# Queued work moved by some ticks, and sums split in halves, in a one-core decoder layer

## The chip, the core and the metric

The kernel is one launch on one core of a Trainium2 chip. Its engines are named as in the profile: PE is TensorE's matrix unit and PEld its weight load, DVE is VectorE, ACT is ScalarE, POOL is GpSimd, and SP issues transfers. SPq, ACTq and POOLq are the transfer queues of these engines. The metric is the device time of one execution in microseconds; lower is better.

## What is computed

One layer of a decoder, for 256 prompt rows and 8 sample rows of one new token each, 264 rows in all, with 2048 channels, in float32:

```python
proj = x @ w_in                                   # 2048 -> all mixer parts
y_a  = ssd(z, conv(xbc), dt, h0)                  # Mamba-2 scan, 32 heads, 4 groups; new state is an output
y_b  = sc_b * dwconv3(sc_c * sc_h)                # short gated convolution
mix  = sigmoid(g_a)*(y_a @ w_branch_ssd) + sigmoid(g_b)*(y_b @ w_branch_sc)
x1   = LN(ALPHA*x + mix @ w_out)
q    = x1 @ w_q                                   # 8 heads, product keys 128 x 128 = 16384 experts
idx, gate = top16 of the sums of two top16 lists, softmax
x2   = LN(ALPHA*x1 + sum_k gate_k * gelu(x1 . u[idx_k]) * v[idx_k])
y    = x2 + sigmoid(x2 @ ple_gate_w) * (p @ ple_proj_w)
```

For 208 of the 264 rows (the "dense" rows, TD = 208) the kernel multiplies x1 with all 16384 rows of u and of v and lays a mostly-zero matrix of gates between the two products; for the other 56 rows (the "sparse" rows, 8 sample rows and 48 prompt rows, shared over 56 gather columns) it gathers the chosen rows of u and v.

## The kernel before

**Weights.** Every product is fed by 128x2048 blocks of weights that come by SP's queue into three tiles (`w`). A half block, 128x1024, is split into a rounded upper part `whi` by ACT (L158) and the rest `wlo` by DVE (L159). PE multiplies both. Four buffers of each part exist up to the stage that scores the keys, five after it, so the two splitting engines can run four to five halves ahead of PE. In the first stages a half is 24 matmuls of 264 columns (L255, L256, L257); in the u and v stages it is 16 matmuls, eight of 416 columns on `whi` (L293 and, for the last block row, L296) and eight of 208 columns on `wlo` (L294).

**Ticks.** The program is written as a list of instructions by Python code that walks through the half blocks. Each half ends with `tick`: functions put down by `defer(n, f)` run n ticks after, and background work, written as generators, goes on. A generator that yields a number spends it from a budget of about 1.1 to 1.3 a tick; one that yields `("w", n)` sleeps n ticks. So the place of every background instruction between the splits of two halves, on each engine's own queue, is set by these numbers. Each engine takes its queue in order.

**Stages**, with the count of halves: convolved inputs (48), short convolution (96), z (32), the two branch products, w_out, w_q (to half 368), u (256 halves, 368 to 624), v (256 halves in eight chunks of 16 blocks), the small product with p (four halves, L1559 to L1561), and the last gate (32).

**What the change touches.**
- `ssd_group` (L551): the scan of one group. L592 takes an exponential of 1024 columns, L595 eight times a relu of 128 columns for each of two chunks, and L598 an exponential again, all on ACT.
- `ssd_samples` (L643): 64 units, one per tick, over a ring of eight buffers `h0t`. A unit's state is loaded by SP's queue, one tick later scaled by ACT (L681), then added to on DVE (L675), then multiplied with C (L665), and stored by POOL's queue in the fourth tick after the load.
- `Norm` (class at L856): the layer norm over the 16 blocks of 128 channels. `pilot` (L874) multiplies the first block with ones for an estimate of the mean; `gather` (L881) takes it off every block and makes the products; `rest` (L923) does the same for the 56 sparse rows, one of 16 blocks after another (L948 on ACT, L952 on DVE), each waiting for that block's `gather`.
- `select` (L1134): the choice of 16 experts per row on DVE, its transposes on PE (L1220, `slt`), `gates` (L1256) which makes the gate matrix from products (`g_mm`, L1279) and stores it to `g_d`.
- `sparse_experts` (L1285): gathers of u's and v's rows by POOL (`ug`, two buffers), a multiply of 2048 columns per gather on DVE (L1363 for u, L1373 for v), and `replicate` (L1304), which lays out x1 by transposes (`x1t`).
- `to_v` (L1517): once the gates are stored and nothing is deferred, it closes the pools of the selection, opens those for v, and starts `prep(0)` (L1432: loads `gl` and `al`, two multiplies, the split `co`) and `residual` (L1495: 16 copies of x1 into `acc`, L1499).
- `v_evac` (L1474): adds each finished product of the v stage to `acc` (L1480, 416 columns: two halves of 208). In the last chunk the two halves of `acc` are folded into one (L1482), and the block goes to the second norm.

## Time and profile before

| what | value |
| --- | --- |
| runs | 2478.10, 2481.56, 2488.36 us; median 2481.56 us |
| the profiled execution | 2488.03 us, of which the span is 2486.3 us |
| mean granted TensorE clock | 0.994 of full speed |
| HBM read, written | 646.32 MB, 39.46 MB, 276 GB/s over the span |
| busy share PE, DVE, ACT, POOL | 98%, 81%, 59%, 24% |

The page of the profile gives busy times and the chain of work that ended last. Beside it stand: the list of waits (`PE mm L294 <- DVE wlo L159: 23.9, 35, 2.8` says that PE's line L294 waited 23.9 us in all, 35 times, 2.8 us at the longest, for DVE's L159); windows, which give each engine's busy time and instructions in a stretch, then the granted clock, the share of the DMA engines, and GB/s; groups of instructions (line, engine, operation, shapes, count | busy us, mean ns of one | idle before it); and the timeline (start, duration, engine, line, operation, and in brackets the idle time before it and what ended it).

### The profile page before, as it was taken

The page shows a single profiled execution, that of the slowest core. Times are in us where ns is not written, and L with a number is a line of the kernel's source. Part 1 is how long each engine was busy: PE and PEld are TensorE (multiplying, and loading weights), DVE is VectorE, ACT ScalarE, POOL GpSimd, SP SyncE. Part 2 cuts the span into 40 slices and gives each one's busy share as a digit, 9 for nine tenths or more (in the row PEclk, how much of TensorE's full clock was granted, in tenths as well). Part 3 has the DMA queues.
Part 4 walks back from the last instruction along what each step waited for, and adds up shares of the span by engine and source line. Part 5 has one row for each costly group of instructions (what it writes and reads, how often), then busy time and mean ns, then how long its engine had stood idle before and what let it go on. Part 6 is the DMA issues. An engine that isn't in the chain of part 4 may idle for free.

```text
span 2486.3 us, 47938 instructions
## 1 busy us (share of the span) xinstructions
PE 2427.8 (98%) x19049; PEld 2399.4 (97%) x19049; DVE 2008.8 (81%) x3192; ACT 1459.5 (59%) x2310; POOL 606.5 (24%) x720
## 2 busy tenths in 40 slices
PE   9999999999999999999999999999999999999989
PEld 9999999999999999998999999999999999999989
DVE  8889865567455578999998778769899999899987
ACT  6776654455444455754777788866544555445564
POOL 2332200000000010100345666632332323323201
PEclk9999999999999999999999999999999999999999
DMA  6788755555555555566779999999999999999554
GB/s 250 250 293 277 256 190 189 199 194 189 201 188 202 190 201 187 195 211 202 243 290 341 357 360 371 370 348 399 394 371 381 383 378 395 364 372 379 200 176 148
DMA packets 137105, 688.91 MB, mean 277 GB/s; under 512 B 15744, under 2 KB 53168, under 8 KB 63280
## 3 DMA queue, kind: packets, MB, share of 16 engines
q1 hardware_dynamic: 89168, 495.46, 55.9%
q0 software_dynamic: 28688, 158.69, 16.5%
q10 hardware_dynamic: 19024, 31.69, 3.5%
q8 instruction: 149, 2.44, 0.4%
q14 instruction: 76, 0.62, 0.1%
HBM read 646.32 MB, written 39.46 MB: 276 GB/s over the span
## 4 chain that ended last, share of the span: by engine, by line
PE 57%; DMA 15%; DVE 15%; issue 6%; ACT 6%; POOL 1%; ACTq 0%; SPq 0%; DVEq 0%; POOLq 0%
PE mm L255 12%; PE mm L257 12%; PE mm L256 12%; PE mm L293 10%; DVE wlo L159 7%; DMA w<-vP 6%; PE mm L294 5%; DMA w<-uT 4%; ACT whi L158 3%; DMA h0t<-h 2%; DVE ug L1363 1%; ACT o L1270 1%; DVE acc L1480 1%; DMA o_hs<-h0t 1%; DMA ug<-vR,sidx 1%
## 5 line engine op out<-in xcount | busy, mean ns | idle before, releaser
L159 DVE TENSOR_TENSOR wlo<-w,whi 128x1024 fp32r<-128x1024 f32 x916 | 1112.3, 1222 | 359.7 <-ACT whi L158 354.1
L158 ACT CAST whi<-w 128x1024 fp32r<-128x1024 f32 x916 | 943.8, 1044 | 611.8 <-DMA w<-vP 249.8
L293 PE MATMUL mm<-x,whi 128*128 128x416 f32 x1920 | 572.8, 365 | 4.1 <-ACT whi L158 4.1
L293 PE MATMUL mm<-co,whi 128*128 128x416 f32 x1920 | 562.1, 361 | 0.0
L255 PE MATMUL mm<-x,whi 128*128 128x264 f32 x1920 | 533.9, 278 | 4.4 <-ACT whi L158 4.4
L257 PE MATMUL mm<-x,wlo 128*128 128x264 f32 x1920 | 532.2, 277 | 5.2 <-DVE wlo L159 5.0
L256 PE MATMUL mm<-x,whi 128*128 128x264 f32 x1920 | 531.1, 277 | 0.0
L294 PE MATMUL mm<-x,wlo 128*128 128x208 f32 x2048 | 505.1, 257 | 16.0 <-DVE wlo L159 15.7
L294 PE MATMUL mm<-co,wlo 128*128 128x208 f32 x2048 | 501.2, 255 | 8.4 <-DVE wlo L159 8.1
L294 PEld LDWEIGHTS mm<-x,wlo 128*128 128x128 f32 x2048 | 392.7, 193 | 26.3 <-DVE wlo L159 25.5
L294 PEld LDWEIGHTS mm<-co,wlo 128*128 128x128 f32 x2048 | 390.6, 192 | 13.8 <-DVE wlo L159 13.7
L257 PEld LDWEIGHTS mm<-x,wlo 128*128 128x128 f32 x1920 | 363.9, 190 | 7.2 <-DVE wlo L159 7.2
L293 PEld LDWEIGHTS mm<-x,whi 128*128 128x128 f32 x1920 | 365.5, 190 | 5.6 <-ACT whi L158 4.4
L255 PEld LDWEIGHTS mm<-x,whi 128*128 128x128 f32 x1920 | 364.2, 190 | 6.2 <-ACT whi L158 4.8
L256 PEld LDWEIGHTS mm<-x,whi 128*128 128x128 f32 x1920 | 364.1, 190 | 0.0
L293 PEld LDWEIGHTS mm<-co,whi 128*128 128x128 f32 x1920 | 363.3, 189 | 0.0
L1269 POOL TENSOR_SCALAR o<-iot,slot,slot 128x128 f32<-128x128 f32 x156 | 184.4, 1188 | 2.7 <-issue 0.9
L1293 POOL DMA_INDIRECT ug<-vR,sidx x56 | 105.5, 1885 | 270.6 <-DVE x1s L1373 227.2
L1293 POOL DMA_INDIRECT ug<-uR,sidx x56 | 92.1, 1644 | 274.3 <-DVE ug L1363 198.2
L1363 DVE SCALAR_TENSOR_TENSOR ug<-ug,x1s 128x2048 f32<-128x2048 f32 x56 | 127.7, 2281 | 2.1 <-DMA ug<-uR,sidx 2.1
L1373 DVE SCALAR_TENSOR_TENSOR x1s<-ug,scf,x1s 128x2048 f32<-128x2048 f32 x53 | 124.1, 2342 | 0.0
L896 POOL CAST r1h<-r1gbh 128x2 fp32r<-128x2 f32 x16 | 7.0, 438 | 439.9 <-DVE mxl L242 439.9
(364 smaller groups left out, 3936.6 us busy)
## 6 DMA issues: line engine op xcount, KB each, us to landing
w<-uT SPq DMA_DIRECT2D x128, 1024.0 KB, 7.2
w<-vP SPq DMA_DIRECT2D x128, 1024.0 KB, 8.9
w<-w_in SPq DMA_DIRECT2D x118, 1024.0 KB, 4.9
w<-w_bc SPq DMA_DIRECT2D x16, 1024.0 KB, 4.9
w<-w_bs SPq DMA_DIRECT2D x16, 1024.0 KB, 4.9
w<-w_o SPq DMA_DIRECT2D x16, 1024.0 KB, 4.9
w<-w_q SPq DMA_DIRECT2D x16, 1024.0 KB, 4.9
w<-w_pg SPq DMA_DIRECT2D x16, 1024.0 KB, 5.0
```

What stands on the lines that cost most here:

```text
L158: ac.copy(hi, w)
L159: ve.tensor_tensor(lo, w, hi.bitcast(F), OP.subtract)
L255: te.matmul(ps, wh, vh, start=(first and q == 0), stop=False)
L256: te.matmul(ps, wh, vl, start=False, stop=False)
L257: te.matmul(ps, wl, vh, start=False, stop=(last and q == n - 1))
L293: te.matmul(ps, hi[:, ws], both, start=(kb == 0), stop=False)
L294: te.matmul(ps[:, :TD], lo[:, ws], one, start=False, stop=False)
L1269: (gp if q < 3 else ve).tensor_scalar(o1[:, q], iot, slot[0][:, c], slot[2][:, c], OP.is_equal, OP.mult)
L1270: ac.activation(o2[:, q], iot, AF.Abs, bias=slot[1][:, c], scale=-1.0)
L1293: gp.indirect_dma_start(out=t, out_offset=None, in_=tab, in_offset=bass.IndirectOffsetOnAxis(ap=sidx[:, c:c + 1], axis=0))
L1363: ve.scalar_tensor_tensor(t, t, 1.0, x1s, OP.mult, OP.mult, accum_out=shid[:, c:c + 1])
L1373: ve.scalar_tensor_tensor(x1s, t, scf[:, c:c + 1], x1s, OP.mult, OP.add)
```

## The change

All parts leave the arithmetic of the result the same but for the order of sums in `v_evac`:
- `ssd_group`: after the first exponential one tick of sleep; relus in groups of two per tick, not four; a tick of sleep after the second exponential.
- `ssd_samples`: ACT's step two ticks after the load, not one, and all later steps of a unit one tick later too.
- `Norm`: `pilot` runs four ticks after the first block (it was one or two); blocks that come before it are kept in a list; POOL's two small copies are issued with the gather; `rest` stays two blocks behind the gathers.
- `select`: three more yields cut its DVE work; the transposes are deferred by five ticks (they waited two), and `gates` starts accordingly.
- `gates`: the products run eight ticks after their factors (six before), and the store ten (eight before).
- `replicate`: a block's transposes come three ticks after its copy, not two.
- `v_evac`: a block's two halves are folded in chunk 2, 3, 4 or 5 (blocks 0 to 3, 4 to 7, 8 to 11, 12 to 15); after that its sum of 416 columns becomes two additions of 208 columns into one half, and the last chunk folds nothing.
- `to_v`: starts seven ticks after its condition holds.

```diff
@@ -590,12 +590,14 @@
 
         ce = ep.tile([128, 8, CH], F, name="ce", tag="arow", bufs=3)
         ac.activation(ce, ar[1], AF.Exp)
+        yield ("w", 1)
         for c in range(2):
             for h in range(8):
                 ac.activation(ar[c][:, h], ar[c][:, h], AF.Relu, bias=tcol[:, c, 8 * g + h:8 * g + h + 1], scale=-1.0)
-                if h % 4 == 3:
+                if h % 2 == 1:
                     yield ("w", 1)
             ac.activation(ar[c], ar[c], AF.Exp, scale=-1.0)
+            yield ("w", 1)
         ve.tensor_tensor(ce, ce, CT[g][:, None, CH:PT].to_broadcast([128, 8, CH]), OP.mult)
         yield 1.1
         yield ("w", 1)
@@ -654,11 +656,11 @@
             return t[s, 512 * g + 256 * a:512 * g + 256 * a + 256, :].rearrange("(q p) n -> p q n", p=128)
 
         u = 0
-        while u < n + 4:
-            if 0 <= u - 4:
-                gp.dma_start(out=rows(o_hs, u - 4), in_=hts.pop(u - 4))
-            if 0 <= u - 3 < n:
-                v = u - 3
+        while u < n + 5:
+            if 0 <= u - 5:
+                gp.dma_start(out=rows(o_hs, u - 5), in_=hts.pop(u - 5))
+            if 0 <= u - 4 < n:
+                v = u - 4
                 g, s, a = units[v]
                 for q in range(2):
                     jk = ab("jk", width=128)
@@ -668,14 +670,14 @@
                     for q in range(4):
                         j = 4 * g + q
                         ve.scalar_tensor_tensor(XS[j][:, PT:], XS[j][:, PT:], col(P_D, j), ysum[:, j], OP.mult, OP.add)
-            if 0 <= u - 2 < n:
-                v = u - 2
+            if 0 <= u - 3 < n:
+                v = u - 3
                 g, s, a = units[v]
                 for q in range(2):
                     ve.scalar_tensor_tensor(hts[v][:, q], bcs[v // 2][:, 0], xds[g][:, 2 * a + q, s:s + 1],
                                             hts[v][:, q], OP.mult, OP.add)
-            if 0 <= u - 1 < n:
-                v = u - 1
+            if 0 <= u - 2 < n:
+                v = u - 2
                 g, s, a = units[v]
                 for q in range(2):
                     ac.activation(hts[v][:, q], hts[v][:, q], AF.Copy, scale=dexp[:, 4 * g + 2 * a + q, 1, s:s + 1])
@@ -870,13 +872,15 @@
             self.d = []
             self.n = 0
             self.acc = None
+            self.first = []
 
         def pilot(self):
             ps = bank("pil")
             te.matmul(ps[:, :self.w], o128, self.s0[:, :self.w], start=True, stop=True)
             self.c = block("pc")
             ac.copy(self.c[:, :self.w], ps[:, :self.w])
-            self.gather(self.s0)
+            for s in self.first:
+                self.gather(s)
 
         def gather(self, s):
 
@@ -888,13 +892,13 @@
             h, l = self.new(self.name)
             hv, lv = halves(h)[:, :, :w // 2], halves(l)[:, :, :w // 2]
             sv = even_odd(s[:, :w])
+            gp.tensor_copy(halves(h)[:, :, T // 2], self.gb[0][:, j])
+            gp.tensor_copy(halves(l)[:, :, T // 2], self.gb[1][:, j])
             q = s[:, w:2 * w] if beside else block("dsq")
 
             def on_act():
                 ac.activation(hv, sv, AF.Copy, scale=col(self.g, j))
                 ac.activation(q, s[:, :w], AF.Square)
-                gp.tensor_copy(halves(h)[:, :, T // 2], self.gb[0][:, j])
-                gp.tensor_copy(halves(l)[:, :, T // 2], self.gb[1][:, j])
                 if j == 0:
                     if beside:
                         a = lp.tile([128, 2, w], F, name="da", tag="as", bufs=2)
@@ -941,7 +945,7 @@
             self.acc.append((a[:, 0], a[:, 1]))
             yield 1.0
             for j in range(16):
-                while self.n <= j:
+                while self.n <= min(j + 2, 15):
                     yield ("w", 1)
                 h, l = (halves(v[j])[:, :, w // 2:T // 2] for v in (self.h, self.l))
                 x = even_odd(xs[:, j])
@@ -957,7 +961,9 @@
         def add(self, s):
             if self.s0 is None:
                 self.s0 = s
-                soon(self.pilot)
+                defer(4, self.pilot)
+            if self.c is None:
+                self.first.append(s)
             else:
                 self.gather(s)
 
@@ -1165,13 +1171,15 @@
         sh = sp.tile([128, w], U32, name="sh", tag="sh", bufs=2)
         ve.tensor_scalar(sh[:n], pu, 2, None, OP.logical_shift_right)
         ve.tensor_copy(ab_f[:n, 3], sh[:n])
+        yield 0.9
         fa, fb = ab_f[:n, 0], ab_f[:n, 1]
         ve.scalar_tensor_tensor(fa, ab_f[:n, 3], -12.0, ab_f[:n, 2], OP.add, OP.max)
         ve.tensor_scalar(ab_f[:n, 2], fa, 4.0, 48.0, OP.mult, OP.add)
         ve.scalar_tensor_tensor(ab_f[:n, 2], fa, 16.0, ab_f[:n, 2], OP.mult, OP.min)
+        yield 0.8
         ve.tensor_copy(fb, pu)
         ve.tensor_tensor(fb, fb, ab_f[:n, 2], OP.subtract)
-        yield 1.4
+        yield 0.5
         HH = max(1, nh // 4)
         for s in range(2):
             af = ab_f[:, s].rearrange("p (h k) -> p h k", h=nh)
@@ -1214,15 +1222,19 @@
                 spawn(sparse_experts(), True)
             if t != 1:
                 nd = min(n, TD - t0)
-                yield ("w", 2)
-                ps = bank("slt")
-                for q in range(3):
-                    te.transpose(ps[:, q * 128:q * 128 + n], sel[:n, q], ident[:n, :n])
-                for q in range(3):
-                    ac.copy(slot[q][:, t0:t0 + nd], ps[:, q * 128:q * 128 + nd])
+
+                def to_slots(t0=t0, n=n, nd=nd, sel=sel):
+                    ps = bank("slt")
+                    for q in range(3):
+                        te.transpose(ps[:, q * 128:q * 128 + n], sel[:n, q], ident[:n, :n])
+                    for q in range(3):
+                        ac.copy(slot[q][:, t0:t0 + nd], ps[:, q * 128:q * 128 + nd])
+                    DONE["slot" + str(t0)] = True
+
+                defer(5, to_slots)
                 if t == 0:
-                    tasks.insert(0, {"gen": gates(t0, nd), "wait": clock["t"] + 1})
-        while "G" + str(PT // 2) not in DONE:
+                    tasks.insert(0, {"gen": gates(t0, nd), "wait": clock["t"] + 6})
+        while "G" + str(PT // 2) not in DONE or "slot0" not in DONE:
             yield ("w", 1)
         yield from gates(0, PT // 2)
 
@@ -1269,9 +1281,9 @@
                 (gp if q < 3 else ve).tensor_scalar(o1[:, q], iot, slot[0][:, c], slot[2][:, c], OP.is_equal, OP.mult)
                 ac.activation(o2[:, q], iot, AF.Abs, bias=slot[1][:, c], scale=-1.0)
             ac.activation(o2, o2, AF.Relu, bias=1.0, scale=-1.0)
-            defer(6, lambda o1=o1, o2=o2, gs=gs, q0=q0: g_mm(o1, o2, gs, q0))
+            defer(8, lambda o1=o1, o2=o2, gs=gs, q0=q0: g_mm(o1, o2, gs, q0))
             if q0 + 4 == tb:
-                defer(8, lambda gs=gs, b0=b0: ac.dma_start(out=g_d[b0] if b0 < NB else gr_d, in_=gs))
+                defer(10, lambda gs=gs, b0=b0: ac.dma_start(out=g_d[b0] if b0 < NB else gr_d, in_=gs))
             yield 0.1
             yield grid(3)
         DONE["G" + str(t0)] = True
@@ -1305,7 +1317,7 @@
 
             k0, n = GR[g]
             t = lp.tile([128, D], F, name="x1s", tag="x1s", bufs=2)
-            for b in range(6):
+            for b in range(7):
                 if b < 4:
                     tb = t[:, b * 512:(b + 1) * 512]
                     x = x1sp[:, 4 * b:4 * b + 4, k0:k0 + n]
@@ -1316,8 +1328,8 @@
                         for h in range(PH):
                             ac.copy(tb.rearrange("p (q h i c) -> p q h i c", q=4, h=PH, i=NS)[:, :, h],
                                     x[:, :, :, None].to_broadcast([128, 4, n, TOPK // NS]))
-                if b >= 2:
-                    tb = t[:, (b - 2) * 512:(b - 1) * 512]
+                if b >= 3:
+                    tb = t[:, (b - 3) * 512:(b - 2) * 512]
                     ps = bank("x1t")
                     for q in range(4):
                         te.transpose(ps[:, q * 128:(q + 1) * 128], tb[:, q * 128:(q + 1) * 128], ident)
@@ -1474,12 +1486,17 @@
     def v_evac(c, db):
         def f(ps):
             a = ACC[db]
+            one = a[:, :TD]
             if c == 0:
                 ve.scalar_tensor_tensor(a, a, ALPHA, ps, OP.mult, OP.add)
+            elif c <= 2 + db // 4:
+                ve.tensor_tensor(a, ps, a, OP.add)
             else:
-                ve.tensor_tensor(a, ps, a, OP.add)
+                ve.tensor_tensor(one, ps[:, :TD], one, OP.add)
+                ve.tensor_tensor(one, ps[:, TD:], one, OP.add)
+            if c == 2 + db // 4:
+                ve.tensor_tensor(one, one, a[:, TD:], OP.add)
             if c == ECH - 1:
-                ve.tensor_tensor(a[:, :TD], a[:, :TD], a[:, TD:], OP.add)
                 n2.add(a)
         return f
 
@@ -1526,13 +1543,19 @@
         return t
 
     nxt = None
+
+    def stored():
+        if "G0" in DONE and not later and "stored" not in DONE:
+            DONE["stored"] = clock["t"] + 7
+        return clock["t"] >= DONE.get("stored", 1 << 30)
+
     for e in range(NE):
         pair_block(x1_p, u_evac(e), 1.1)
-        if nxt is None and "G0" in DONE and not later:
+        if nxt is None and stored():
             nxt = to_v()
     while nxt is None:
         tick(1.2)
-        if "G0" in DONE and not later:
+        if stored():
             nxt = to_v()
     while len(ACC) < KB:
         tick(1.2)
```

**Place 1, ACT in the first scan group.** `h0t` is a unit of the sample ring, `arow` the rows of the scan's decays, `ce` the exponential. Before:

```order
L681 ACTIVATE h0t<-h0t,dexp 128x128 x2
L592 ACT_TABLE_LOAD
L592 ACTIVATE ce<-arow 128x1024
L595 ACTIVATE arow<-arow,tcol 128x128 x4
L158 CAST whi_91<-w 128x1024
L732 COPY scc<-mm 128x264
L681 ACTIVATE h0t<-h0t,dexp 128x128 x2
L595 ACTIVATE arow<-arow,tcol 128x128 x4
L158 CAST whi_90<-w 128x1024
```

Changed:

```order
L683 ACTIVATE h0t<-h0t,dexp 128x128 x2
L592 ACT_TABLE_LOAD
L592 ACTIVATE ce<-arow 128x1024
L158 CAST whi_91<-w 128x1024
L734 COPY scc<-mm 128x264
L683 ACTIVATE h0t<-h0t,dexp 128x128 x2
L596 ACTIVATE arow<-arow,tcol 128x128 x2
L158 CAST whi_90<-w 128x1024
```

The four relus that stood between the exponential and the split are gone from there, and two now stand ahead of each following split.

**Place 2, DVE and ACT where u ends and v begins.** L1478 (L1491 in the change) adds v's first finished block; `x1s` is the sum of the gathered rows, `as` the product with u, `al` and `co` are v's factors being prepared. DVE before:

```order
L159 TENSOR_TENSOR wlo_94<-w,whi_90 128x1024
L1373 SCALAR_TENSOR_TENSOR x1s<-ug,scf,x1s 128x2048
L159 TENSOR_TENSOR wlo_13259<-w,whi_13258 128x1024
L1408 TENSOR_TENSOR as<-mm,as 128x208
L159 TENSOR_TENSOR wlo_97<-w,whi_93 128x1024
L159 TENSOR_TENSOR wlo_95<-w,whi_92 128x1024
L1478 SCALAR_TENSOR_TENSOR acc<-acc,mm 128x416
```

DVE changed:

```order
L159 TENSOR_TENSOR wlo_13259<-w,whi_13258 128x1024
L1420 TENSOR_TENSOR as<-mm,as 128x208
L1454 TENSOR_TENSOR al<-al,gl 128x4x192
L1455 TENSOR_TENSOR al<-al,gl 128x4x16
L1466 TENSOR_TENSOR co<-al,co 128x8x104
L1385 SCALAR_TENSOR_TENSOR x1s<-ug,scf,x1s 128x2048 x2
L159 TENSOR_TENSOR wlo_97<-w,whi_93 128x1024
L1385 SCALAR_TENSOR_TENSOR x1s<-ug,scf,x1s 128x2048
L159 TENSOR_TENSOR wlo_95<-w,whi_92 128x1024
L1491 SCALAR_TENSOR_TENSOR acc<-acc,mm 128x416
```

ACT changed, at the same place:

```order
L158 CAST whi_13258<-w 128x1024
L1419 COPY as<-mm 128x208
L1423 ACTIVATE as<-as 128x416
L1424 DMA a_d<-as 128x416
L1516 COPY acc<-x_12367 128x2x2x104 x2
L1465 CAST co<-al 128x8x104
L1516 COPY acc<-x_12514 128x2x2x104 x4
L1516 COPY acc<-x_12661 128x2x2x104 x4
L158 CAST whi_93<-w 128x1024
```

`to_v` starts 16 ticks later (tick 602, not 586), so the copies of `residual` are not finished when the u stage ends at half 624: the loop that waits for 16 tiles of `acc` goes through nine ticks without a half, and their background work (ten copies, a split of `co`, three sums) stands between the splits of two halves. Before, these copies stood two by two between splits of the u stage.

**Place 3, ACT in the last chunk of v.** L894 and L895 (L900 and L901) are the `gather` of a block, L948 (L952) the step of `rest`. Before:

```order
L158 CAST whi_91<-w 128x1024
L894 ACTIVATE r_26205<-acc,cpar 128x2x104
L895 ACTIVATE acc<-acc 128x208
L948 ACTIVATE r_26205<-x1sp,cpar 128x2x28
L158 CAST whi_90<-w 128x1024
```

Changed:

```order
L158 CAST whi_91<-w 128x1024
L900 ACTIVATE r_26255<-acc,cpar 128x2x104
L901 ACTIVATE acc<-acc 128x208
L952 ACTIVATE r_26049<-x1sp,cpar 128x2x28
L158 CAST whi_90<-w 128x1024
```

The step of `rest` works on another pair of blocks than the gather just ahead of it; before, on the same.

## The prediction, made before the changed kernel ran

> **What bounds the kernel now.** I read the clocks first, then the busy times, then what PE waits for. Page and clock:
>
> ```profile
> PE 2427.8 (98%) x19049; PEld 2399.4 (97%) x19049; DVE 2008.8 (81%) x3192; ACT 1459.5 (59%) x2310; POOL 606.5 (24%) x720
> core 0: 2486.3 us, clock 0.994
> ```
>
> PE is busy 98%: the change leaves its matmuls alone, so it can only touch what PE loses, 2486.3 − 2427.8 = 58.5 us of idle time, and the clock, 0.6% or about 15 us. PE's waits (us in total, times, longest):
>
> ```profile
> PE mm L294 <- DVE wlo L159: 23.9, 35, 2.8
> PE mm L1559 <- DVE acc L1480: 7.2, 2, 4.9
> PE mm L257 <- DVE wlo L159: 5.0, 8, 0.8
> PE mm L255 <- ACT whi L158: 4.4, 2, 3.4
> PE mm L293 <- ACT whi L158: 4.1, 1, 4.1
> PE slt L1220 <- DVE sel L1199: 3.0, 2, 1.9
> PE pil L876 <- DVE acc L1482: 2.0, 1, 2.0
> PE x1t L1323 <- ACT x1s L1313: 1.0, 1, 1.0
> ```
>
> These are 50.6 us, all of them waits for DVE or ACT, none for a transfer directly. Where they fall, by windows (span, then busy PE, PEld, DVE, ACT, POOL, then granted clock, DMA share, GB/s):
>
> ```profile
> 170.00:190.00 20.00, 16.06 (x112) 15.36 (x112) 13.09 (x44) 12.74 (x27) 2.43 (x5) 0.83 0.83 296
> 190.00:270.00 80.00, 76.00 (x669) 73.48 (x668) 72.41 (x223) 53.11 (x113) 21.56 (x38) 1.00 0.83 271
> 1160.00:1180.00 20.00, 16.38 (x96) 15.16 (x96) 19.18 (x56) 7.37 (x11) 0.00 (x0) 0.91 0.60 206
> 1660.00:1680.00 20.00, 15.31 (x87) 14.54 (x86) 6.14 (x6) 7.97 (x13) 5.22 (x7) 0.83 0.83 317
> 1680.00:1760.00 80.00, 78.57 (x541) 77.41 (x540) 73.53 (x74) 50.04 (x74) 25.37 (x20) 1.00 1.00 400
> 2216.80:2290.80 74.00, 73.81 (x514) 73.48 (x513) 68.04 (x71) 35.29 (x37) 20.34 (x17) 1.00 0.97 378
> 2290.80:2370.50 79.70, 74.94 (x520) 73.23 (x519) 75.59 (x117) 41.78 (x73) 22.50 (x43) 1.00 0.62 219
> 2370.00:2390.00 20.00, 12.75 (x83) 12.16 (x81) 13.94 (x22) 12.23 (x27) 2.81 (x9) 0.74 0.56 192
> ```
>
> So there are four sore places: the scan (170 to 270), the selection (near 1170), `to_v` (near 1670), and the last chunk of v with what follows (2290 to 2390). After each longer wait the granted clock falls: (1 − clock) x 20 us is 3.4, 1.8, 3.4 and 5.2 us. A chunk of v without trouble is 74.0 us for 32 halves, 2.31 us a half.
>
> **The change part by part.** Gains are counted against the profiled execution.
>
> *A, scan and samples.* ACT at the first scan group:
>
> ```profile
> 177.18 1.28 ACT L592 ACT_TABLE_LOAD   x1
> 178.48 1.06 ACT L592 ACTIVATE ce<-arow 128x1024 f32<-128x1024 f32 x1
> 179.44 1.26 ACT L595 ACTIVATE arow<-arow,tcol 128x128 f32<-128x128 f32 x4
> 180.61 1.03 ACT L158 CAST whi<-w 128x1024 fp32r<-128x1024 f32 x1
> 181.69 0.59 PE L255 MATMUL mm<-x,whi 128*128 128x264 f32 x1 [3.39 <-ACT whi L158]
> ```
>
> The relus (1.26 us) leave this place; a table load and exponential stay, 2.3 us, ahead of the split. The sample's scale was just before, and with two ticks from the load it can arrive. In all 4.4 (L255) + 4.0 (80 − 76.00) + 3.4 of clock = 11.8 us are here. I take 9; from 5 (the relus and half of the clock) to 11.
>
> *B, selection.* Its DVE instructions ran ahead of two splits in a row, and PE waited:
>
> ```profile
> 1172.37 2.35 DVE L159 TENSOR_TENSOR wlo<-w,whi 128x1024 fp32r<-128x1024 f32 x2
> 1173.63 0.36 PE L294 MATMUL mm<-x,wlo 128*128 128x208 f32 x1 [2.77 <-DVE wlo L159]
> ```
>
> The yields cut that run (20 − 16.38 = 3.6 us and 1.8 of clock), five ticks' delay takes the wait of `slt` (3.0), three ticks that of `x1t` (1.0): 9.4 us. DVE was 19.18 of 20 us busy there, so some of the work only moves to the next split: I take 6, from 3 to 8.5. By the Trainium skill, "TensorE: Matmul & The Clock Gate", Part 1, the clock halves after an idle window of about 3.4 us; a wait of 2.77 us would then cost no clock, and B would be 4. The row of 1160 to 1180 has 0.91, so here the trace decides against it.
>
> *C, `to_v` taken from where it was.* It waited for the store of the gates:
>
> ```profile
> 1671.71 1.01 ACT L1499 COPY acc<-x 128x416 f32<-128x416 f32 x2 [10.98 <-DMA g_d<-gs]
> 1673.70 0.72 PE L293 MATMUL mm<-x,whi 128*128 128x416 f32 x1 [4.14 <-ACT whi L158]
> ```
>
> ACT stood 10.98 us in its queue, with the splits behind it; PE lost 20 − 15.31 = 4.7 and 3.4 of clock, 8.1 us. Seven ticks are 7 x 2.31 = 16 us, longer than the 10.98, so all 8.1 come back.
>
> *D, what `to_v` costs where it now ends.* Nine ticks without a half stand between the stages (place 2 of the order). The rows for it are from the u and v stages (gathers and copies; for `ug` the last number is us to landing):
>
> ```profile
> ug<-vR,sidx POOLq DMA_INDIRECT x56, 11.2
> L1373 DVE SCALAR_TENSOR_TENSOR x1s<-ug,scf,x1s 128x2048 f32<-128x2048 f32 x19 | 44.5, 2342 | 0.0
> L1499 ACT COPY acc<-x 128x416 f32<-128x416 f32 x16 | 8.4, 583 | 11.4 <-DMA g_d<-gs 11.0 <-ACT as L1411 0.4
> L1453 ACT CAST co<-al 128x832 fp32r<-128x832 f32 x4 | 3.9, 974 | 0.4 <-ACT as L1411 0.4
> ```
>
> On ACT ten copies and a split of `co` are 10 x 0.5 + 1.0, about 6 us and with `as` 8, ahead of a split. On DVE there are three sums of 2.34 us; two of them wait for gathers that POOL can only start once the sum before last has freed its buffer, 11.2 us each. PE has four halves split ahead, 4 x 2.31 = 9.2 us. ACT's 8 fit into that. For DVE the first sum waits for nothing much, the second for its gather, some 11.2 + 2.3 after the stretch begins, the third for the next one, which overlaps half: about 19 us until the last split is free, less 9.2, so about 10 us lost and 3.4 of clock as at the two places with a 3.4 to 4.1 us wait. I take a loss of 13; from 5 (half of the 10, if a gather has landed before, and no clock) to 19 (14 and 5.2 of clock, as in the last row of the windows).
>
> *E, halves in the v sums.* 56 sums become two, and the folds go from chunk 7 to chunks 2 to 5:
>
> ```profile
> L1480 DVE TENSOR_TENSOR acc<-mm,acc 128x416 f32<-128x416 f32 x33 | 19.2, 582 | 0.0
> L1482 DVE TENSOR_TENSOR acc<-acc 128x208 f32<-128x208 f32 x14 | 5.2, 374 | 0.5
> ```
>
> A pair costs 2 x 0.374 − 0.582 = 0.17 us more, four folds 1.5. Chunks 2 to 6 get 1.5, 2.2, 2.8, 3.5 and 2.7 us of DVE work each; chunk 6 has 74.0 − 68.04 = 6.0 us free. On average it fits; where a gather's sum, a product and a split meet, it may not. I take a loss of 4, from 0 to 8 (two thirds of the 12.7).
>
> *F, last chunk and p's product.* A loop between ACT, DVE and PE:
>
> ```profile
> 2371.10 0.43 DVE L910 SCALAR_TENSOR_TENSOR r<-acc,cpar,r 128x208 fp32r<-128x208 f32 x1 [0.20 <-POOL r L897]
> 2371.57 0.35 ACT L948 ACTIVATE r<-x1sp,cpar 128x56 fp32r<-128x56 f32 x1 [1.21 <-DVE r L910]
> 2371.82 1.97 ACT L158 CAST whi<-w 128x1024 fp32r<-128x1024 f32 x2
> 2380.51 0.59 PE L1559 MATMUL mm<-pp,whi 128*128 128x264 f32 x1 [4.91 <-DVE acc L1480]
> ```
>
> ACT's step of `rest` waits 1.21 us for the product of the very same block (L910), and two splits stand behind it; DVE's split waits for these, and L910 of the next block stands behind that. `rest` two blocks behind takes the wait out; folds (16 x 0.374 = 6.0 us, less 16 x 0.17 = 2.7) leave DVE, the sparse sums end some 15 ticks earlier, and POOL's copy is issued before it is waited for. What is lost here: 79.70 − 74.94 = 4.8 in chunk 7 (the 2.0 of `pil` in it), 7.25 and 5.2 of clock behind: 17.2 us. I take 17, from 8 (half, if DVE stays at 75.59 of 79.70) to 17.2.
>
> *Sum*: 9 + 6 + 8 − 13 − 4 + 17 = 23 us. The profiled execution took 2488.0 us, so 2465; the median of the runs is 6.5 below it, so **2458.5 us**. Ends: 11 + 8.5 + 8 − 5 − 0 + 17.2 = 40 gives 2442; 5 + 3 + 8 − 19 − 8 + 8 = −3 gives 2484.
>
> **The rivals.**
>
> 1. *The boundary of u and v is not covered.* The nine ticks are 9 x 2.31 = 20.8 us of work; if its gathers leave no cover, PE loses all, and some 10 of clock (the two worst windows together, 5.2 + 3.4, and a little): 31 and not 13. Then 23 − 18 = 5: 2476. For it: three sums stand ahead of a split (place 2). Against: 9.2 us of splits are ahead.
>
> 2. *Transfers are the bound from 1680 to 2290.* The windows show a DMA share of 0.97 to 1.00. If what PE gains there it waits for in weights, C's 8 are given back: 15 us, 2466. For it: share 1.00 at 400 GB/s; against: no wait of PE is for a late weight, and 2216 to 2290 runs at 73.81 of 74.0. The Trainium skill, "DMA: Bandwidth & Descriptors" (the note on 436 and about 360), has the HBM side bind at about 358 GB/s, so v's stage should long be bound by it; 400 GB/s in the window does not agree.
>
> 3. *Slower: the samples' ring.* A load on SP waits for the store of the unit eight before, and that store is a tick later:
>
> ```profile
> SPq L692 <- DMA o_hs<-h0t: 13.1, 15, 2.2
> o_hs<-h0t POOLq DMA_DIRECT2D x64, 128.0 KB, 5.0
> h0t<-h SPq DMA_DIRECT2D x64, 128.0 KB, 5.3
> ```
>
> A half there is 24 matmuls of 80/669 us, 2.87; eight are 23 us. If the added tick enters the round of a buffer, which waits already, each of 8 rounds is up to 2.9 us longer, and the weight loads that stand behind on SP with it; a wait of that length cost 1.8 us of clock near 1173. So 8 x 4.7 = 37 us go in place of A's gain of 9: 23 − 9 − 37 = −23, and the median is 2481.6 + 23, about 2505. It decides once a round (5.3 + 5.0 and the steps between) is longer than eight halves. Against: scale and store stay three ticks apart, and the load runs ahead of PE, so the extra tick only gives the load room.
>
> 4. *The tail does not do what it says*: ACT's wait for L910 goes, but DVE, 75.59 of 79.70 busy, binds the loop in its place. F then gives the folds' 3.3 us and the `pil` alone, about 5 of 17: 2471.
>
> **How the numbers follow.** Chances: the forecast 0.62, rivals 1 to 4: 0.12, 0.10, 0.06, 0.10. The bound for "same" is 0.5% or 12.4 us, about what a measurement of this kernel can tell from no change: 2469 to 2494. Faster: 0.95 of the forecast's 0.62, most of rival 2, and a third of 1 and 4, about 0.75; slower 0.06, rival 3 and little else; same 0.19. The range is 2443 to 2478: it takes in the ends of the sum but for the worst, rivals 1, 2 and 4, and leaves out rival 3.
>
> **What would show it right or wrong.** A: L255's 3.4 us wait is gone, the clock from 170 to 190 is 1.00, and L692's wait for `o_hs` stays near 13 us (rival 3: it grows to over 30). B: no wait of L1220; the 2.77 at L294 near 1173 is below 1. C: no 10.98 us on L1499. D: between the last u half and the first of v a wait of L294 or L293 of 5 to 15 us with L1385's sums before it, and a window of 20 us there at 0.8; without it I am too high by 13, with 20 or more rival 1 holds. E: L294's waits from 1830 to 2290 rise by 2 to 6 us. F: L1559 no longer waits, the 74% clock is gone; if it still waits on DVE, rival 4. The sum is wrong if the gain at 2290 to 2390 is under 8 us or the boundary costs over 20.

## The result, and the profile after

The changed kernel takes 2496.69 us (median of 8 runs, 2488.61 to 2500.22) against 2481.44 us for the kernel before (8 runs): ratio 1.0058, 95% interval 1.0041 to 1.0075. It is slower by about 14 us; 2458.5 was forecast, 0.991. The profiled execution took 2498.82 us, 10.8 more than that of before. Chips differ by some us, so below each kernel's ratio to the kernel before, run beside it, is given; 0.1% is 2.5 us.

Page and clock of the changed kernel:

```profile
PE 2428.1 (97%) x19049; PEld 2395.6 (96%) x19049; DVE 2015.9 (81%) x3248; ACT 1458.7 (58%) x2310; POOL 643.5 (26%) x720
core 0: 2496.7 us, clock 0.996
```

Its list of PE's waits (us in all, times, longest), the first five:

```profile
PE mm L294 <- DVE wlo L159: 37.9, 44, 4.3
PE mm L257 <- DVE wlo L159: 9.7, 13, 1.8
PE mm L293 <- DVE co L1466: 7.6, 1, 7.6
PE mm L1582 <- DVE acc L1496: 2.5, 1, 2.5
PE mm L255 <- ACT whi L158: 1.4, 4, 0.4
```

Most of the waits that were to go did go: L255's 3.4 us, `slt`, `pil`, `x1t`, L293 for ACT's split, and 4.7 of L1559's 7.2 (now L1582). The clock even rose, from 0.994 to 0.996. But L294 waits 14 us longer for DVE, L257 4.7, and a wait of 7.6 us for `co` is new.

PE takes the same 17,888 products with a weight block in the same order in both kernels. So the lag of the change can be read off at any place: the start of the same matmul in its timeline, less the start in that of before. Here and below, a lag at half n, from 464 on, is read at the last matmul of half n + 1, so that a stop at the start of half 592 or in half 625 counts to the stretch that ends at 592 or at 624. A gain is how much the lag falls over a stretch. Each lag is read from one execution.

| stretch | lag at its end, us | gain, us | forecast |
| --- | --- | --- | --- |
| up to the scan (86 us) | +0.3 | −0.3 | 0 |
| scan, samples, all up to u | +1.5 | −1.2 | A: 9 |
| u, to half 464 (selection) | −5.8 | +7.3 | B: 6 |
| u, halves 464 to 584 | +3.8 | −9.6 | 0 |
| halves 584 to 592 (the old `to_v`) | −2.2 | +6.0 | C: 8 |
| halves 592 to 640 (new `to_v`, the boundary) | +19.9 | −22.0 | D: −13 |
| v, halves 640 to 848 | +27.8 | −8.0 | E: −4 |
| last chunk to the end | +10.4 | +17.4 | F: 17 |

Three rows are as forecast (B, C, F). A gave nothing, D cost 9 more, 10 us went where no term stood, and v lost 8 where 4 stood.

**Scan.** In the change, SP's wait at a sample's load and ACT's wait for weights, from 86 to 470 us:

```profile
SPq L694 <- DMA o_hs<-h0t: 86.8, 19, 8.2
ACT whi L158 <- DMA w<-w_in: 27.4, 12, 4.5
```

The first was 13.1 us in 15 stops; the second did not occur. SP takes its queue in order, and weight loads stand behind a sample's load that waits for its buffer. The window from 90 to 290 us, of before and then of the change:

```profile
90.00:290.00 200.00, 191.35 (x1672) 187.15 (x1672) 181.45 (x562) 143.11 (x317) 63.23 (x120) 0.98 0.86 283
```

```profile
90.00:290.00 200.00, 189.66 (x1653) 185.01 (x1652) 178.46 (x556) 142.03 (x310) 63.80 (x118) 1.00 0.86 281
```

The clock is whole now, and yet PE gets 19 matmuls less done in the same time.

**Boundary.** In the change, the timeline rows that stop DVE and PE, and two windows:

```profile
1722.34 1.04 ACT L158 CAST whi<-w 128x1024 fp32r<-128x1024 f32 x1 [3.84 <-DMA w<-uT]
1725.05 0.96 DVE L1454 TENSOR_TENSOR al<-al,gl 128x768 f32<-128x768 f32 x1 [6.48 <-DMA al<-a_d]
1727.34 0.54 PE L294 MATMUL mm<-x,wlo 128*128 128x208 f32 x1 [4.30 <-DVE wlo L159]
...
1764.53 2.35 DVE L159 TENSOR_TENSOR wlo<-w,whi 128x1024 fp32r<-128x1024 f32 x2
1769.05 0.92 ACT L1465 CAST co<-al 128x832 fp32r<-128x832 f32 x1
1769.86 3.81 ACT L1516 COPY acc<-x 128x416 f32<-128x416 f32 x8
1770.00 1.03 DVE L1466 TENSOR_TENSOR co<-al,co 128x832 fp32r<-128x832 f32 x1 [1.84 <-ACT co L1465]
1771.08 0.72 PE L293 MATMUL mm<-co,whi 128*128 128x416 f32 x1 [7.58 <-DVE co L1466]
1774.58 2.35 DVE L1385 SCALAR_TENSOR_TENSOR x1s<-ug,scf,x1s 128x2048 f32<-128x2048 f32 x1 [1.29 <-DMA ug<-vR,sidx]
1779.24 2.35 DVE L1385 SCALAR_TENSOR_TENSOR x1s<-ug,scf,x1s 128x2048 f32<-128x2048 f32 x1 [1.18 <-DMA ug<-vR,sidx]
...
1715.00:1735.00 20.00, 15.70 (x92) 15.34 (x92) 11.17 (x12) 9.15 (x12) 5.99 (x8) 0.83 0.96 347
1755.00:1785.00 30.00, 22.03 (x130) 21.23 (x129) 24.84 (x22) 17.95 (x26) 11.17 (x11) 0.83 0.91 346
```

There are two stops, not one. The first, inside the u stage, is the first product of `prep`: DVE stands 6.48 us in its queue for a load of `al`, with the splits behind it. The second is PE's wait for the last `co`, which is made in the empty ticks (ticks between u and v in which no half is split). The splits were not late there: DVE had made two at 1764.53, and the sums that wait for gathers (1.29 and 1.18 us) come behind `co`. Each stop costs clock too, 0.17 of 20 and of 30 us, which is 3.4 and 5.1 us; with the waits of 4.30 and 7.58 these are 20 of the 22 us.

**In v**, the same kind of stop comes once more (POOL, then DVE; the window from 1920 to 2290 below):

```profile
2080.67 2.81 POOL L1305 DMA_INDIRECT ug<-vR,sidx  x1 [4.98 <-DVE x1s L1385]
2084.93 0.58 POOL L1441 DMA_DIRECT2D al<-a_d  x1
2100.02 0.96 DVE L1454 TENSOR_TENSOR al<-al,gl 128x768 f32<-128x768 f32 x1 [7.53 <-DMA al<-a_d]
1920.00:2290.00 370.00, 361.68 (x2509) 358.55 (x2509) 350.06 (x400) 178.04 (x211) 110.43 (x102) 1.00 0.97 378
```

A chunk's first load stood behind a gather on POOL that waited for its buffer, and then took 15 us to land; DVE's product comes four ticks (9.2 us) after the load's place.

**Tail**, PE's waits from 2290 us to the end in the change:

```profile
PE mm L1582 <- DVE acc L1496: 2.5, 1, 2.5
PE mm L1582 <- ACT pj L1589: 0.4, 1, 0.4
```

Before, these were 11.8 us (7.2, 2.6 and 2.0).

### The profile page after: what moved, and what is told of

It reads as the page before. It is cut to its first block, busy times and chain, and to the rows that moved or that the text cites. A ratio compares the mean times of both kernels' runs of the same rounds, so it can differ in the third digit from the quotient of the medians.

```text
span 2496.7 us, 47975 instructions
## 1 busy us (share of the span) xinstructions
PE 2428.1 (97%) x19049; PEld 2395.6 (96%) x19049; DVE 2015.9 (81%) x3248; ACT 1458.7 (58%) x2310; POOL 643.5 (26%) x720
## 5 line engine op out<-in xcount | busy, mean ns | idle before, releaser
L293 PE MATMUL mm<-x,whi 128*128 128x416 f32 x1920 | 572.0, 364 | 1.0 <-ACT whi L158 0.8
L293 PE MATMUL mm<-co,whi 128*128 128x416 f32 x1920 | 564.7, 363 | 7.6 <-DVE co L1466 7.6
L257 PE MATMUL mm<-x,wlo 128*128 128x264 f32 x1920 | 532.5, 277 | 9.8 <-DVE wlo L159 9.7
L255 PE MATMUL mm<-x,whi 128*128 128x264 f32 x1920 | 533.8, 278 | 1.5 <-ACT whi L158 1.4
L294 PE MATMUL mm<-x,wlo 128*128 128x208 f32 x2048 | 505.6, 257 | 27.1 <-DVE wlo L159 26.9
L294 PE MATMUL mm<-co,wlo 128*128 128x208 f32 x2048 | 502.9, 256 | 11.2 <-DVE wlo L159 11.1
L294 PEld LDWEIGHTS mm<-x,wlo 128*128 128x128 f32 x2048 | 392.8, 193 | 39.3 <-DVE wlo L159 38.7
L294 PEld LDWEIGHTS mm<-co,wlo 128*128 128x128 f32 x2048 | 393.1, 193 | 16.5 <-DVE wlo L159 16.3
L257 PEld LDWEIGHTS mm<-x,wlo 128*128 128x128 f32 x1920 | 363.7, 189 | 12.9 <-DVE wlo L159 12.8
L293 PEld LDWEIGHTS mm<-co,whi 128*128 128x128 f32 x1920 | 365.2, 190 | 7.9 <-DVE co L1466 7.8
L293 PEld LDWEIGHTS mm<-x,whi 128*128 128x128 f32 x1920 | 365.0, 190 | 3.5 <-ACT whi L158 2.4
L255 PEld LDWEIGHTS mm<-x,whi 128*128 128x128 f32 x1920 | 363.7, 189 | 4.1 <-ACT whi L158 2.7
L1281 POOL TENSOR_SCALAR o<-iot,slot,slot 128x128 f32<-128x128 f32 x156 | 229.1, 1475 | 14.6 <-issue 4.9
L1305 POOL DMA_INDIRECT ug<-vR,sidx x56 | 98.8, 1765 | 284.0 <-DVE x1s L1385 231.4
L895 POOL CAST r1h<-r1gbh 128x2 fp32r<-128x2 f32 x16 | 7.5, 469 | 443.7 <-DVE mxl L242 443.7
```

What stands on the lines that cost most here:

```text
L255: te.matmul(ps, wh, vh, start=(first and q == 0), stop=False)
L257: te.matmul(ps, wl, vh, start=False, stop=(last and q == n - 1))
L293: te.matmul(ps, hi[:, ws], both, start=(kb == 0), stop=False)
L294: te.matmul(ps[:, :TD], lo[:, ws], one, start=False, stop=False)
L1281: (gp if q < 3 else ve).tensor_scalar(o1[:, q], iot, slot[0][:, c], slot[2][:, c], OP.is_equal, OP.mult)
L1305: gp.indirect_dma_start(out=t, out_offset=None, in_=tab, in_offset=bass.IndirectOffsetOnAxis(ap=sidx[:, c:c + 1], axis=0))
```

## The experiments

Results are ratios to the kernel before with their 95% intervals; us are worked out from them with 2481.

**The change less one part** (e1 to e3), and the norm alone on the kernel before (e4).

e1, all stages of `ssd_samples` as before:

```diff
-            if 0 <= u - 2 < n:
-                v = u - 2
+            if 0 <= u - 1 < n:
+                v = u - 1
```

> The change with the five stages of the sample units put back as before (scale one tick after the load); all else changed. Theory 1, the ring: SP waited 86.8 us in 19 stops for stores of the sample ring (13.1 in 15 before), and ACT then 27.4 us for weights (0 before). Put back, SP's wait falls to under 25 us, ACT's wait for w<-w_in in the scan to under 5, and the stretch from the scan to the end of z gains 4 to 9 us: 2488 to 2493 us. Rival, DVE: the scan loses its time because DVE's split is late for DVE's own work; then the waits of L257 for wlo stay at 8 to 10 us and the time stays at 2495 to 2499.

1.0020 (0.9997 to 1.0042), 9 us less than the change; up to the u stage its trace is 7.0 us ahead of the change's. SP's wait falls to 32.1 us, ACT's wait for weights to none, L257's to 2.2. Theory 1 holds, SP's wait a little above its mark.

e2, `to_v` at once:

```diff
-        if nxt is None and stored():
+        if nxt is None and "G0" in DONE and not later:
```

> The change without the seven ticks of delay ahead of to_v; all else changed. Theory 1, the boundary: the ticks without a half between u and v and the late loads of prep cost 18 us (lag of the change against before, from 1700 to 1790 us of the span). With fewer such ticks, 7.6 us of L293 waiting for co and 4.3 of L294 go, and at most the 4.1 us wait for the store of the gates and 3.4 of clock come back: 2484 to 2489 us. Rival: the time between 1440 and 2290 is set by the transfers (DMA share 0.93 to 0.98), so what is gained here is lost behind it: 2494 to 2499.

0.9999 (0.9987 to 1.0011), 15 us less, more than theory 1 said. `to_v` comes at tick 594 (the old one came at 586, since the gates are later in the change), two ticks stay empty in place of nine, PE no longer waits for `co`, ACT not for `g_d`, and the first `al` lands 1.7 us ahead of its product.

e3, whole sums in v and the fold in the last chunk:

```diff
-            elif c <= 2 + db // 4:
+            else:
                 ve.tensor_tensor(a, ps, a, OP.add)
...
+            if c == ECH - 1:
+                ve.tensor_tensor(a[:, :TD], a[:, :TD], a[:, TD:], OP.add)
```

> The change with whole sums of 416 columns in v and the fold in the last chunk, as before; all else changed. Theory 1: the halves cost 7 to 8 us in chunks 4 and 5 (L294 waiting for wlo near 2038, 2099, 2104 and 2143 us) and save 3 in chunk 7: 2490 to 2494 us. Rival, phase: these waits come from where the gathers fall after the boundary, not from the halves; then the same number of waits stays, in other places, and with the folds back in chunk 7 the time is 2497 to 2503.

1.0060 (1.0039 to 1.0080): no difference that can be measured. The loss from half 640 to 848 stays, 7.7 us of 8.0. So it is not the halves', as the rival said.

e4, on the kernel before, all of the change in the class `Norm` and nothing else:

```diff
-                while self.n <= j:
+                while self.n <= min(j + 2, 15):
...
-                soon(self.pilot)
+                defer(4, self.pilot)
```

> The kernel before with the norm's part alone (pilot four ticks after, POOL's copies with the gather, rest two blocks behind). Theory 1: the loop of ACT's L948 and DVE's L910 is what lost the tail, so the two waits of L1559 (7.2 us) and the low clock of 5.2 us go, without any fold moved: 10 to 14 us faster, 2467 to 2471. Rival, DVE binds the last chunk: without the folds moved out of it the wait turns into one for DVE's acc, and only 3 to 6 us are gained: 2475 to 2479.

0.9972 (0.9957 to 0.9986), 7 us, at the edge of the rival's range: L1563 (the same matmul) still waits 4.7 us for DVE's sums, of 7.2 before. So the norm's order gives less than half of what the tail of the change shows.

**The ring, and the late load** (e5, e6).

e5 keeps the new stages and gives the ring a ninth buffer:

```diff
-                h = ep.tile([128, 2, 128], F, name="h0t", tag="h0t", bufs=8)
+                h = ep.tile([128, 2, 128], F, name="h0t", tag="h0t", bufs=9)
```

> The change with nine buffers in the ring of the samples, not eight; nothing else differs, so the scale stays two ticks after the load. Theory 1, the ring: one more buffer gives the store the tick back that the change took, SP's wait for o_hs falls from 87 us to under 25, ACT's wait for w<-w_in in the scan from 27 to under 5, and the time up to the u stage is 5 to 9 us less, like that of the kernel with the old sample stages. Ratio to before 0.997 to 1.003, where the change had 1.0058. Rival: it is the later order of DVE's and ACT's work that costs, not the buffer; then SP's wait falls and the time up to the u stage stays within 2 us of the change's, ratio 1.005 to 1.007.

1.0003 (0.9993 to 1.0013), 14 us less. The rows of e5:

```profile
SPq L694 <- DMA o_hs<-h0t: 28.6, 21, 3.4
ACT whi L158 <- DMA w<-w_in: 6.1, 3, 3.1
90.00:290.00 200.00, 198.16 (x1757) 195.82 (x1756) 189.55 (x589) 149.20 (x323) 65.15 (x126) 1.00 0.90 296
```

PE gets 104 matmuls more done in this window than in the change, and 85 more than before: with room in the ring, the relus and the scale in their new places do win what A said, 10.6 us up to the u stage against before. SP's and ACT's waits stay a little above their marks (25 and 5). The place is the same in all traces: the five other kernels with nine buffers are 8.9 to 10.8 us ahead of before at the start of the u stage, while the ten with the new stages and eight buffers, the change among them, lie between 4.3 ahead and 3.3 behind.

e6 issues a chunk's first load with the chunk before:

```diff
-            if k % 4 < 3:
+            if k + 1 < 4 * ECH:
                 load(k + 1)
```

> The change with the first load of gl and al of each chunk of v issued together with the chunk before (and so without the four ticks of waiting ahead of it); the seven ticks ahead of to_v and the nine ticks without a half stay. Theory 1, late loads: in v DVE stood 7.5 us at the product of al in chunk 4 (load issued behind a gather on POOL and 15 us under way), and the loss of 8 to 12 us between 1920 and 2290 is this and its like; it goes, and PE is busy for all but 3 us of these 370: ratio 1.001 to 1.003. Rival: the waits come from the share of the DMA engines (0.97) whatever the order, and only move: PE's idle time from 1920 to 2290 stays at 6 to 10 us, ratio 1.005 to 1.007.

1.0026 (1.0015 to 1.0038), 8 us less. The window of e6:

```profile
1920.00:2290.00 370.00, 366.28 (x2539) 362.59 (x2538) 355.29 (x404) 179.95 (x214) 104.70 (x96) 1.00 0.97 378
```

PE idles 3.7 us there and not 8.3, at the same DMA share of 0.97: the late load cost it, not the share. That is worth about 4 us: by lag, halves 640 to 848 lose 4.3 us and not 8.0. The trace also gains 4.5 us on the change's ahead of the u stage and 3.8 between halves 464 and 584, where the edit changes nothing, and loses 3.4 more from 592 to 640, so the 8 us of the ratio are not all shown to be the load's.

**The selection part** (e7, and e13 to e15).

e7, `select`, `gates` and `replicate` all as before, so among others:

```diff
-                defer(5, to_slots)
+                yield ("w", 2)
...
-            defer(8, lambda o1=o1, o2=o2, gs=gs, q0=q0: g_mm(o1, o2, gs, q0))
+            defer(6, lambda o1=o1, o2=o2, gs=gs, q0=q0: g_mm(o1, o2, gs, q0))
...
-            for b in range(7):
+            for b in range(6):
```

> The change with select, gates and replicate as before (yields, transposes two ticks after, products after six ticks and the store after eight). Theory 1: these parts win 5 to 8 us near 1170 and 1230 to 1330 and lose as much between 1500 and 1600, where weights and gathers are late; so without them the time stays, ratio 1.004 to 1.008, with the 2.8 us wait near 1170 back and less than 2 us of L294's waits from 1444 to 1661. Rival: the loss near 1500 to 1600 is not theirs (the samples or the norm shift the gathers); then it stays and the ratio grows to 1.008 to 1.011.

0.9970 (0.9959 to 0.9981): faster than either theory, which had missed that the earlier gates bring `to_v` back to tick 594 and leave two empty ticks. Against e2, which has `to_v` there too, 0.3% remain, 7 us, as a cost of the selection part itself: the loss between halves 528 and 560, about 5 us in e1, e2, e3, e5 and e6, is not in e7.

Where it comes from was asked three ways: e13 has the third of these edits, e14 the second, e15 the first, each with `to_v` held at tick 602 (a delay of 11 ticks in place of 7).

> The change with replicate as before (transposes two ticks after the copy, six ticks in all, so the gathers start one tick earlier) and the delay ahead of to_v set so that it stays at tick 602. Theory 1, the start of the gathers: the 5 us that each kernel with the whole selection part lost between halves 528 and 560 come from the gathers being one tick later against the gate factors on POOL; they go, ratio 1.002 to 1.0045. Rival, the sum of parts: neither replicate nor any one part of the selection does it; ratio 1.005 to 1.0065, with L294 waiting 4 to 7 us between 1444 and 1661.

> The change with the gate products at six and the store at eight ticks as before, to_v held at tick 602. Theory: late gate products hold POOL's factors (4.4 us of waiting for PE) and with them the gathers; without them the 5 us between halves 528 and 560 go, ratio 1.002 to 1.0045. Rival: not they; ratio 1.005 to 1.0065, the waits of L294 between 1444 and 1661 still 4 to 7 us.

> The change with select as before (old yields, transposes two ticks after), to_v held at tick 602. Theory: select moves the gates and with them the gathers by some ticks; without it the gain of 5 us between halves 408 and 440 goes and the loss of 5 between 528 and 560 too: ratio 1.005 to 1.0065. Rival: the loss stays and the gain goes, ratio 1.007 to 1.009.

e13: 0.9998 (0.9982 to 1.0014). e14: 1.0022 (1.0009 to 1.0035). e15: 1.0024 (1.0008 to 1.0039). Each part taken out wins 8 to 15 us, none with all the marks foretold. By lag, the loss between halves 528 and 560 is 3.6 us in e13, 2.6 in e14, and gone in e15, which also lost half of the gain near half 432. But single traces differ here: e9 below, with the whole selection part, loses 3.4. Over halves 464 to 584 the nine kernels with the whole part lose 2.8 (e9) to 10.4 us (e16), and e13 loses 3.1; only e14, e15 and e7 lie outside, winning 2.1, 1.2 and 5.8. In e13's trace 5.8 us of what it gains on the change stand ahead of the u stage, where its edit does nothing. So this stretch tells for `gates` and `select`, not for `replicate`. From 1444 to 1661 us, most of these halves, the row of before, then that of the change:

```profile
1444.00:1661.00 217.00, 215.86 (x1547) 214.59 (x1546) 174.68 (x193) 177.45 (x309) 135.64 (x101) 1.00 0.97 371
ACT whi L158 <- DMA w<-uT: 14.6, 9, 3.9
```

```profile
1444.00:1661.00 217.00, 210.40 (x1499) 207.61 (x1498) 163.47 (x181) 171.57 (x304) 155.13 (x105) 1.00 0.93 353
ACT whi L158 <- DMA w<-uT: 23.3, 9, 6.2
```

The DMA engines are busy 0.93 and not 0.97, weights come later, and POOL is busier. Which order of gathers and loads does this was not found; the parts do not add here.

**A boundary with its work hidden** (e8, e9, e16).

e8 is the kernel before with the norm's part, `to_v` five ticks after the store, `residual` first, and e6's early load:

```diff
+            DONE["stored"] = clock["t"] + 5
...
-        spawn(residual())
+        spawn(residual(), True)
```

> A new kernel from the one before: the norm's part of the change, to_v five ticks after the gates' store was issued (11.5 us, where ACT's copy waited 10.98), residual's copies first among the background tasks, so that they end at half 603 and no tick without a half is left, and the first load of a chunk issued with the chunk before. Theory 1: it keeps what the norm alone won (ratio 0.9972), gains 4 to 8 us where ACT waited for the gates' store, and pays nothing between u and v: ratio 0.993 to 0.996. Rival, transfers bind from 1444 to 2290: what is gained at to_v is waited for in weights, ratio 0.997 to 0.999.

0.9943 (0.9928 to 0.9957): theory 1. The copies end at half 603, no tick is empty, ACT and DVE wait for no `g_d` and no `al`, and PE for no `co`.

e9 is the change with the edit `spawn(residual(), True)` alone, so four empty ticks and not nine, at the same tick 602. 

> The change with one word different: residual stands first among the background tasks, so its 16 copies end at half 613 and only prep's last part is left at half 624; four ticks without a half are left there, where the change has nine; to_v stays at tick 602. Theory 1, the empty ticks: the nine cost 17 to 19 us between halves 592 and 624 and four cost 5 to 10, so 7 to 13 us come back, ratio 1.0005 to 1.003, and the 7.6 us wait of L293 for co stays, since prep is as late as before. Rival: the cost there is all prep's (its load of al 6.5 us late and the last co), not the copies'; then 0 to 4 us come back, ratio 1.004 to 1.006.

1.0039 (1.0026 to 1.0051): 5 us, between the two, and nearer the rival. From half 592 to 624 it lost 17.2 us, as much as the change (17.6), and its wait for `co` stayed:

```profile
PE mm L293 <- DVE co L1466: 6.4, 1, 6.4
```

What it won at the boundary, 4.9 us, came behind half 624.

e16 is e2 with the same edit: no empty tick, `to_v` at 594. 

> The change without the delay and with residual first: to_v at tick 594, no tick without a half between u and v (two in the kernel without delay, ratio 0.9999; four in the one with residual first at tick 602, 1.0039). Theory 1, late work: what costs is prep being late at tick 602, not the copies; so removing the last two empty ticks gains 0 to 4 us against 0.9999: ratio 0.998 to 1.000. Rival, the number of empty ticks: about 2 us each, four or five more are gained, and the wait of L293 for ACT there (1.3 us) goes: ratio 0.9965 to 0.998.

0.9982 (0.9968 to 0.9996), 4 us below e2. So five empty ticks less at 602 gave 5 us, two less at 594 gave 4, each near the limit of what these runs can tell, and the place (602 or 594) most of the rest: 10 us between e9 and e2. The count of empty ticks is the smaller part of the price; the late place of `to_v`, and with it of `prep`, is the larger. It shows in the timeline, where DVE makes the four `co` of v's first chunk: while PE is at halves 597, 603, 609 and 614 before, at 603, 609, 613 and 619 in e2, but at 612, 617, 623 and 625 in the change and at 612, 616, 623 and 625 in e9, whose copies came first. PE needs them from half 624 on.

**Towards a better kernel** (e10 to e12, e17, e18). e10 is e8 with the change's `ssd_group` and `ssd_samples` and `bufs=9`; e11 adds the change's `select`, e12 its `gates` in place of that, both with a delay of 4 ticks, `to_v` at 594 and no empty tick.

> The covered-boundary kernel (ratio 0.9943) with the change's scan and sample stages and nine buffers in the ring. Theory 1: with the ninth buffer these stages won 10.6 us up to the u stage against the kernel before, where the covered-boundary kernel was 2.9 ahead; so 6 to 9 us more, ratio 0.990 to 0.992. Rival, phase: the sampled gains of up to 10 us in the scan are swallowed by transfers later, from 1444 on; ratio 0.993 to 0.995.

> The kernel of the run before with the change's select (three more yields, transposes five ticks after) and to_v four ticks after the store; the gate products stay at six and eight ticks. Theory 1: select wins 5 to 8 us between halves 400 and 464, as it did in the change, and it is the gate products at eight and ten ticks that lose 4 to 6 us between 528 and 560 (POOL waits for PE's products, 4.4 us, and for slots, 3.5, ahead of gathers): ratio 3 to 6 us below that of the run before. Rival: the loss between 528 and 560 is select's; then the time is within 2 us of the run before, with the waits of L294 from 1444 to 1661 at 4 to 7 us.

> The covered-boundary kernel with ring and scan, and the change's gates (products eight, store ten ticks after) but the old select; to_v four ticks after the store. Theory 1: the gate products at eight ticks bring the loss between halves 528 and 560: 3 to 6 us slower than without them, L294's waits from 1444 to 1661 at 4 to 7 us, and POOL's gate factors wait for PE again. Rival: select is the cause; then the time is within 2 us of that without, and no wait of PE from 1444 to 1661 is over 2 us in all.

e10: 0.9885 (0.9869 to 0.9902), better than foretold. e11: 0.9881 (0.9865 to 0.9898), 2453.73 us, no difference to e10 that can be measured, so the 3 to 6 us that theory 1 gave to `select` do not show. e12: 0.9907 (0.9891 to 0.9924), 5 us slower than e10, as theory 1 had it, but not where: between halves 528 and 560 it loses 0.9 us, and from 592 to 624 7.8 where e10 lost 4.7. PE's waits in e11, the first three:

```profile
PE mm L294 <- DVE wlo L159: 12.6, 23, 1.4
PE mm L1577 <- DVE acc L1492: 4.8, 2, 3.7
PE mm L257 <- DVE wlo L159: 4.0, 7, 0.8
```

L294 waits half as long as in the kernel before, and never over 1.4 us.

e17 is the whole change with the edits of e5, e6 and e16. 

> The change with its two found faults taken out and all else in it: nine buffers in the ring of the samples, to_v at tick 594 with residual first (no empty tick), and the first load of a chunk issued with the chunk before. Theory: ring (0.55%), place of to_v with no empty tick (0.76%) and early load (up to 0.32%) add up: from 1.0058 to 0.990 to 0.993; what is left to the best kernel so far (0.9881) is the gate products and replicate. Rival, no sum: the place of the gathers decides, and parts do not add; 0.994 to 0.998.

0.9907 (0.9892 to 0.9922): as the theory had it. The ring, the place of `to_v` and the late loads are 1.5% of the time of before, 37 us; singly they were 0.55, 0.76 (e16) and 0.32.

e18 is e11 with the halves. 

> The best kernel so far (select, scan and ring of nine, norm, covered boundary; 0.9881) with the change's halves of the v sums. Theory: in the tail L1577 waits 4.8 us for the last chunk's sums; with the folds gone it waits 2.5 and the last chunk is 2 to 4 us shorter, while chunks 3 to 6 pay 0 to 3: ratio 0.986 to 0.9885. Rival: the halves cost in v what they save in the tail, as in the change: 0.988 to 0.990, no difference that can be measured.

0.9879 (0.9863 to 0.9894): neutral again. L1582 waits 3.5 us where L1577 waited 4.8. By lag the last chunk and what follows win 1.6 us against e11, and halves 640 to 848 lose 0.8.

## Why the prediction was wrong

By the table, of the 23 us that were forecast as a gain A's 9 did not come, the boundary took 9 more than D, v 4 more than E, C gave 2 less, and 9.6 us went in the u stage, for which the sum had nothing. Three steps failed: the ring was counted as no cost, the new place of `to_v` as no cost beyond the empty ticks, and the new order of the selection as no cost behind the waits that it ends.

**A** was right in its own sum: the sample's scale "can arrive" with two ticks from its load, and the term had the right size (9, and e5 against before 10.6 us up to u). What failed is in rival 3, where the way it could go wrong was written down and set aside with "scale and store stay three ticks apart, and the load runs ahead of PE, so the extra tick only gives the load room". The tick stands between a load and its store. So a store comes five ticks after its load, and the load of the unit eight on, whose place in SP's queue did not move, comes three ticks after that store, 3 x 2.87 = 8.6 us, and not four, 11.5. A store needs 5.0 us to land and its issue waited for DVE before. The load waits, and with it the weights that stand behind it. SP's mark for rival 3 ("over 30") came out as 86.8. Its price, 37 us, was too high, also for the clock, which it had falling in each round and which stayed whole (1.00 from 90 to 290 us); the ninth buffer gave back 14 us. Its chance, 0.06, was too low, since the reason against it did not hold. So A's term was right but for the ring, which was counted as nothing.

**B** was right in its place: 7.3 us by half 464, 6 forecast. But the price of the selection's new order further on, 9.6 us between halves 464 and 584, had no term. The prediction followed the delays of `slt` and of the gate products to the waits that they end, and not to the gathers and weight loads that they shift in a stretch with a DMA share of 0.97. e7, e14 and e15 show that the cost hangs on these parts; its mechanism stays open, and its size differs from trace to trace (2.8 to 10.4 us with the same selection part).

**C** came out as 6 of 8.1.

**D** had the right place, the wrong cause for the stop there, and a stop missing. The second stop (7.58 us at PE and 5.1 of clock) is within the 5 to 19 that was forecast, but the working had DVE's splits late behind sums that wait for gathers. These waits were 1.29 and 1.18 us, far below the 11.2 assumed, and the splits were ahead; PE waited for the last `co`, for which the working had no time. So it is luck that 12.7 us came where 13 was forecast. Missing is the first stop, DVE's 6.48 us for `al`, which landed some 15.7 us after its issue (1709.37 us), and cost PE 4.30 and 3.4 of clock. The margin for it could be read in the view of transfers of the kernel before (KB each, median us to landing):

```profile
al<-a_d POOLq DMA_DIRECT2D x32, 416.0 KB, 12.0
```

A first load has four ticks, 9.2 us, by its place, and lands in 12.0 at the median: it is in time only where POOL issues it early. In the kernel before DVE waited for it once, 1.1 us. The change moved `prep` to a place in the round of gathers where it is late, in u and again in chunk 4; e6 gives the first loads of the later chunks more lead. The working also took the place of `to_v` as free: moving it by 16 ticks left `prep` no time, and e2, e9 and e16 show that this, more than the copies, is the price.

**E**: the 8.0 us lost there are not the halves', which cost nothing that can be measured, where 4 was forecast and 0 the lower bound: e3 and e18 have them neutral in sum; of what v lost from half 640 to 848, 8.0 us, the early loads of e6 leave 4.3.

**F** was right in size, 17.4 of 17, but not all of it by its own working: e4, the norm alone, wins 7 us. Part of the rest is lent by the empty ticks: in them the background ran on while PE stood, so the last sum of a gather starts while PE is at half 842 and not 857. Without empty ticks it starts at halves 853 to 858, and the stretch from half 848 to the end is 9.1 to 11.9 us shorter than before (e11, e16, e17, e18), not 17.4.

**Rivals 1, 2 and 4**: PE lost 22 us from half 592 to 640, so half way between the forecast's 13 and rival 1's 31 (with the clock); the prediction's own sign that its sum is wrong, a boundary of over 20, came true. Rival 2 fell: the 12.1 us that e5 gains on the change up to u are still 10.7 at the end of its trace, though the DMA share of v is 0.97. Rival 4 fell: L1559's waits went from 7.2 to 2.5, and F's amount came.

The direction was missed because three costs that were each held to be covered or not counted (the ring, the late `prep` with its loads, the shift of gathers) came together. With ring, boundary and late loads mended, the same change gives 0.9907 (e17), just the ratio that was forecast; but the mends are no part of the change, so this shows the size of the faults, not that the sum was right.
